# Split Gelu-multiply: the first tile loaded in pieces of 1, 3 and 4 rows instead of 4 and 4, and its first four rows computed in steps of 1 and 3

**Chip, cores, metric.** One core of one Trainium2 chip (trn2). The time is device microseconds of one execution; spans come from the hardware profile of one execution and are 1.8 to 2.4 us shorter than its time.

## The reference

```python
x: (32, 512, 2048) float32
x1, x2 = x[..., :1024], x[..., 1024:]
gelu_x1 = 0.5 * x1 * (1 + erf(x1 / sqrt(2)))
return (gelu_x1 * x2).astype(float32)          # (32, 512, 1024)
```

134.22 MB are read, 67.11 MB written, and there is one Gelu and one multiply for each output element.

## The kernel before

16 tiles; a tile has 128 partitions with 8 rows each, so a load is 8.39 MB (64 KB on each partition) and a store 4.19 MB (32 KB on each partition). There are two buffers for input tiles and two for output tiles. Loads go out on the SyncE queue, stores on the ScalarE queue, except those of the last two tiles, which go out on the SyncE queue.

```python
    xpool = ctx.enter_context(tc.tile_pool(name="xpool", bufs=2))
    opool = ctx.enter_context(tc.tile_pool(name="opool", bufs=2))

    def load(i):
        x_tile = xpool.tile([P, R, dim], x.dtype, name="x_tile")
        for rows in (slice(0, 4), slice(4, 8)) if i == 0 else (slice(0, 8),):
            nc.sync.dma_start(out=x_tile[:, rows, :], in_=x_t[i][:, rows, :])
        return x_tile
    # ... (store() cut)
    ahead = [load(0), load(1)]
    for i in range(n_tiles):
        x_tile = ahead.pop(0)
        o_tile = opool.tile([P, R, half], out.dtype, name="o_tile")
        last = i == n_tiles - 1
        pieces = i == 0 or last
        steps = ((0, 2), (2, 4), (4, 8)) if pieces else ((0, 8),)
        for lo, hi in steps:
            rows = slice(lo, hi)
            # Gelu on ScalarE (kept in program order): o_tile[rows] <- x_tile[rows, :half]
            # multiply on VectorE: o_tile[rows] <- o_tile[rows] * x_tile[rows, half:]
            # ...
            if pieces and hi % 4 == 0:
                store(nc.sync if last else nc.scalar, i, o_tile, slice(hi - 4, hi))
        if not pieces:
            store(nc.sync if i == n_tiles - 2 else nc.scalar, i, o_tile, slice(0, R))
        if i + 2 < n_tiles:
            ahead.append(load(i + 2))
```

## Time and profile before

| | before |
|---|---|
| time, median of 6 runs (lowest to highest) | 471.02 us (470.97 to 471.08) |
| span of the profiled run | 469.2 us |
| bytes moved, mean rate | 201.33 MB, 429 GB/s |
| the two DMA queues, share of 16 engines | 70.4% + 29.1% |
| VectorE / ScalarE busy | 30% / 24% |
| first store issued | 19.28 us |

The fourth and fifth rows are the ones to read together: the transfers fill the span (70.4% + 29.1%), and the engines that compute wait for them. The lines themselves are quoted in the prediction below.

### The profile page before, as it was taken

The numbers are of one execution on the slowest core, as the hardware profiler recorded it, in microseconds if no ns is written. First come the engines' busy times: TensorE is split into PE (matmuls) and PEld (weight loads), VectorE is DVE, ScalarE is ACT, GpSimd is POOL, SyncE is SP. The second block draws the span as 40 slices with busy tenths as digits, with TensorE's granted clock in tenths as the row PEclk, the third lists the DMA queues.
The fourth block names the chain that finished last, engine by engine and source line by source line (L and its number), as shares of the span: only waits on it lengthen the run. The fifth ranks groups of instructions, "written<-read, shape, count | busy, mean of one in ns | idle before, by whom it ended". The sixth has DMA issues, their size and how long they took to land.

```text
span 469.2 us, 182 instructions
## 1 busy us (share of the span) xinstructions
DVE 139.5 (30%) x20; ACT 114.2 (24%) x21; POOL 0.2 (0%) x4
## 2 busy tenths in 40 slices
DVE  0330332407033070330704307042070520605142
ACT  1320505041050410505005050050501405014060
POOL 0000000000000000000000000000000000000000
DMA  8999999999999999999999999999999999999998
GB/s 358 447 447 447 402 400 495 402 402 447 481 413 402 447 402 492 402 422 427 492 402 402 447 481 413 402 447 430 464 402 425 425 492 402 402 447 492 402 402 358
DMA packets 5040, 201.33 MB, mean 429 GB/s; under 512 B 560, under 2 KB 560, under 8 KB 560
## 3 DMA queue, kind: packets, MB, share of 16 engines
q1 hardware_dynamic: 2880, 142.61, 70.4%
q10 hardware_dynamic: 2160, 58.72, 29.1%
HBM read 134.22 MB, written 67.11 MB: 429 GB/s over the span
## 4 chain that ended last, share of the span: by engine, by line
DMA 72%; DVE 14%; ACT 12%; ACTq 0%; SPq 0%; issue 0%
DMA out_dram<-o_tile 62%; DVE o_tile L65 14%; ACT o_tile L61 12%; DMA x_tile<-in_x_dram 10%; ACTq L101 0%; SPq L45 0%
## 5 line engine op out<-in xcount | busy, mean ns | idle before, releaser
L65 DVE TENSOR_TENSOR o_tile<-o_tile,x_tile 128x8192 f32<-128x8192 f32 (+2 forms) x20 | 139.5, 6985 | 321.2 <-ACT o_tile L61 321.2
L61 ACT ACTIVATE o_tile<-x_tile 128x8192 f32<-128x8192 f32 (+2 forms) x20 | 112.9, 5661 | 341.3 <-DMA out_dram<-o_tile 303.6
L61 ACT ACT_TABLE_LOAD x1 | 1.3, 1283 | 0.7 <-PEq L90 0.7
L90 POOL MEMSET const-bfloat16-1.0<- 128x1 bf16 x1 | 0.1, 102 | 0.0
L90 POOL MEMSET const-uint8-127<- 128x1 uint8 x1 | 0.1, 102 | 0.0
L90 POOL MEMSET const-float32-1.0<- 128x1 f32 x1 | 0.1, 99 | 0.0
L90 POOL MEMSET const-float32-0.0<- 128x1 f32 x1 | 0.1, 98 | 0.2 <-issue 0.2
## 6 DMA issues: line engine op xcount, KB each, us to landing
out_dram<-o_tile ACTq DMA_DIRECT2D x13, 4096.0 KB, 42.2
x_tile<-in_x_dram SPq DMA_DIRECT2D x2, 4096.0 KB, 16.7
out_dram<-o_tile ACTq DMA_DIRECT2D x2, 2048.0 KB, 34.4
out_dram<-o_tile SPq DMA_DIRECT2D x1, 4096.0 KB, 22.7
out_dram<-o_tile SPq DMA_DIRECT2D x2, 2048.0 KB, 7.7
x_tile<-in_x_dram SPq DMA_DIRECT2D x15, 42.1
```

Of the source, the lines that this page charges most:

```text
L61: nc.scalar.activation(out=o_tile[:, rows, :], in_=x_tile[:, rows, :half], func=GELU)
L65: nc.vector.tensor_mul(out=o_tile[:, rows, :], in0=o_tile[:, rows, :], in1=x_tile[:, rows, half:],)
L90: nc = _bacc.Bacc("TRN2", target_bir_lowering=False, num_devices=1)
```

## The change

Its intent is to have the first row on the chip earlier, to start computing sooner and so to send the first store sooner. The core of the diff:

```diff
+    FIRST = (0, 1), (1, 4), (4, 8)
...
-        for rows in (slice(0, 4), slice(4, 8)) if i == 0 else (slice(0, 8),):
-            nc.sync.dma_start(out=x_tile[:, rows, :], in_=x_t[i][:, rows, :])
+        for lo, hi in FIRST if i == 0 else ((0, 8),):
+            nc.sync.dma_start(out=x_tile[:, lo:hi, :], in_=x_t[i][:, lo:hi, :])
...
-        steps = ((0, 2), (2, 4), (4, 8)) if pieces else ((0, 8),)
+        if i == 0:
+            steps = FIRST
+        else:
+            steps = ((0, 2), (2, 4), (4, 8)) if last else ((0, 8),)
```

The store of rows 0 to 3 still waits for all four of them.

## The prediction

> **What bounds the kernel now.** I read the page first, its 40 slices and its DMA rows, then the chain that ended last, then the timeline of the first 31 us, where the change acts, then the groups by shape for durations, and last some windows, to see whether the transfers ever pause.
>
> ```profile
> DMA  8999999999999999999999999999999999999998
> GB/s 358 447 447 447 402 400 495 402 402 447 481 413 402 447 402 492 402 422 427 492 402 402 447 481 413 402 447 430 464 402 425 425 492 402 402 447 492 402 402 358
> ...
> q1 hardware_dynamic: 2880, 142.61, 70.4%
> q10 hardware_dynamic: 2160, 58.72, 29.1%
> HBM read 134.22 MB, written 67.11 MB: 429 GB/s over the span
> ```
>
> The DMA engines are at nine tenths or more in 38 of 40 slices, and the two queues together took 70.4 + 29.1 = 99.5% of the 16 engines' span. VectorE (30% on the page) and ScalarE (24%) are mostly idle. So the kernel looks bound by bytes: 201.33 MB.
>
> ```profile
> 1.64 45.41 DMA x_tile<-in_x_dram
> 47.05 0.02 issue
> 47.07 7.04 ACT o_tile L61
> 54.11 0.02 issue
> 54.13 8.70 DVE o_tile L65
> 62.84 0.02 issue
> 62.86 37.73 DMA out_dram<-o_tile
> ```
>
> The chain alternates a transfer, a Gelu, a multiply and a store's landing to the end of the span. It looks like a dependency chain, and one might hope to shorten its first link. But its links of 37 to 45 us are transfers that stand in line behind other transfers: a 4.19 MB store alone would need 9.7 us at 432 GB/s. The steady state has two loads and two stores outstanding, so this chain is the queue's own length, told another way. Whether that is so is decided by whether the DMA ever runs dry, and this is the view that decides it:
>
> ```profile
> 2.00:468.40 466.40, 139.53 (x20) 112.96 (x21) 0.00 (x0) 1.00 1.00 431
> 454.00:466.00 12.00, 5.93 (x2) 2.29 (x1) 0.00 (x0) 1.00 1.01 434
> ```
>
> The columns are stretch, length, busy VectorE, ScalarE and GpSimd, TensorE clock, DMA share, GB/s. The share is 1.00 over all but the first two microseconds and the last one, and it is still 1.01 in the tail, where only stores are left. The trace keeps a record of each packet; following them engine by engine I find no pause longer than 0.06 us on any of the 16 between the first packet, 1.75 us into the span, and the last, which ends at 467.9. So the span is 1.75 us of start, 466.1 us of unbroken transfer, and about 1.3 us after the last packet. The median time of 471.01 us is 1.8 us more than the 469.2 us span.
>
> **The first tile.**
>
> ```profile
> 12.81 3.71 ACT L61 ACTIVATE o_tile<-x_tile 128x2048 f32<-128x2048 f32 x2 [10.80 <-DMA x_tile<-in_x_dram]
> 14.75 4.49 DVE L65 TENSOR_TENSOR o_tile<-o_tile,x_tile 128x2048 f32<-128x2048 f32 x2 [14.75 <-ACT o_tile L61]
> 19.28 0.38 ACTq L49 DMA_DIRECT2D out_dram<-o_tile  x1
> 22.52 3.62 ACT L61 ACTIVATE o_tile<-x_tile 128x4096 f32<-128x4096 f32 x1 [6.00 <-DMA x_tile<-in_x_dram]
> ```
>
> Rows 0 to 3 land at 12.79, and their store is issued at 19.28. Rows 4 to 7 land at 22.50, which is 9.71 us later: 4.19 MB / 9.71 us = 432 GB/s, across a border between two DMAs, so that border cost nothing visible. Until 19.28 the queue is never short of work: the second half of tile 0 and all of tile 1 (8.39 MB, landing at 47.05) wait behind the first piece.
>
> **What the Trainium skill says.** "DMA: Bandwidth & Descriptors", section "Issuing engines are not separate DMA queues", says that DMAs started by any engine run on the same 16 DMA engines and interleave. The trace agrees: the load queue and the store queue add up to 99.5%, so an earlier store takes time from a load. "Perfetto Trace Analysis", section "DMA Optimizations", says that splitting lets work start sooner, and gives as the condition that the DMA engines are generally idle. Here they are not. "ScalarE: Activation LUTs", section "What ACT_TABLE_LOAD costs", gives 186 ns + 0.833 N ns for an activation with immediate scale and bias, 1892 ns at N = 2048; the mean here is 1900. "VectorE: DVE Perf Modes", in its section on the TRN2 errata, gives (N+151)/0.96 ns for an fp32 tensor_tensor, 2291 ns at 2048; the mean here is 2288. Both agree, and I use durations from these rows:
>
> ```profile
> L65 DVE TENSOR_TENSOR o_tile<-o_tile,x_tile 128x2048 f32<-128x2048 f32 x4 | 9.0, 2288 | 30.0 <-ACT o_tile L61 30.0
> L65 DVE TENSOR_TENSOR o_tile<-o_tile,x_tile 128x4096 f32<-128x4096 f32 x2 | 8.9, 4426 | 7.7 <-ACT o_tile L61 7.7
> L61 ACT ACTIVATE o_tile<-x_tile 128x2048 f32<-128x2048 f32 x4 | 7.4, 1900 | 32.8 <-DMA out_dram<-o_tile 22.0 <-DMA x_tile<-in_x_dram 10.8
> L61 ACT ACTIVATE o_tile<-x_tile 128x4096 f32<-128x4096 f32 x2 | 7.2, 3608 | 6.0 <-DMA x_tile<-in_x_dram 6.0
> ```
>
> **The change part by part.** It removes from tile 0 two Gelus and two multiplies of 2048 elements, and adds one of 1024 and one of 3072 on each engine. The lines through the rows above give 192 + 0.834 N ns for the Gelu and 150 + 1.044 N ns for the multiply. So the Gelus become 1.05 and 2.75 us, and the multiplies 1.22 and 3.36 us; the sums, 3.80 and 4.58 us, are those of before (3.80 and 4.58) within rounding, since the instruction count does not change.
>
> Row 0 is a quarter of the first piece: it lands 7.28 us before the four rows did (3.15 MB / 432), at about 5.5 us. Its Gelu and multiply are over by about 7.8 us, 5 us before rows 1 to 3 are there. Those land where the four rows did, at about 12.85. Then Gelu 12.87 to 15.62, multiply 15.64 to 19.00, store issued at about 19.02, against 19.28: **0.26 us earlier**. That small gain is because the multiply of rows 1 to 3 can't start before its whole 3072-element Gelu is through; in the kernel before, the second Gelu ran beside the first multiply. Taking one row out ahead saves 1.05 us of the Gelus after landing and 1.2 us of the multiplies, but loses most of it again by less overlap. The second step of tile 0 waits for its own load at 22.5 and does not move, nor does the third load's issue at about 30.6, which waits for the last multiply of tile 0.
>
> What are 0.26 us worth? While the queue is full, a store that comes sooner only pushes a load's packets back by as much. The total of transfer time is unchanged: **gain on the path 0.0 us**.
>
> Cost: one more load DMA. It brings 128 packets, 8 on each engine, and one small semaphore packet on each. Packets of 16, 32 and 64 KB have medians of 611, 1213 and 2418 ns in the packet records, so doubling the size falls short of doubling the time by about 8 ns: that is the fixed part of a packet. Then 8 and 24 KB take about 310 and 912 ns instead of one of 32 KB at 1213: 9 ns x 8 = 72 ns per engine, plus one semaphore packet of about 9 ns: **+0.08 us**, all of it on the path since no engine pauses. The third issue on the SyncE queue, about 0.4 us, moves tile 1's load from 1.64 to about 2.05; it has 8.39 MB ahead of it, so that is hidden. The sum is 471.01 + 0.08 = 471.1 us.
>
> **Rivals.** (a) *The earlier store carries through to the end*, as the intent and the chain of waits suggest: 471.01 - 0.26 = 470.7 us. For it: the chain starts with the first loads. Against it: DMA share 1.00. (b) *The small first piece breaks the stream*: between the issue at 0.73 us and the landing at 12.79 there are 12.06 us for 9.71 us of bytes, so a start and receipt cost 2.3 us; if a further DMA paid some of it unhidden, 472 to 473 us. Against it: the border between the two pieces now shows no gap, and the second issue is over at about 1.6 us, when the first piece still has some 3 us to run. (c) *A bubble in the tail*: stores get ahead of loads, the last load lands later than 449.05, and the last store (issued at 460.80) finds an empty queue. At 460.80 there were about (467.9 - 460.8) x 432 = 3.07 MB left, of which 2.10 are that last store; the other 0.97 MB are 2.2 us of work, against about 1.0 us from an issue to its first packet (0.73 to 1.75). That leaves 1.2 us of slack; a store that starts 0.26 us earlier can shift the loads by no more than 0.26 us. So no bubble; if there were one, a few tenths at most.
>
> **Range and chances.** All rivals but (b) lie within 0.4 us. The three times of before spread over 0.11 us. I add something for differences between executions: 471.1 us, 470.6 to 471.6. A 2% change is 9.4 us; nothing here is of that size, and the whole time outside unbroken transfer is about 5 us. Same 0.99.
>
> **What would show it.** Right: 5184 packets (4608 of data, 576 small) with 3024 on the load queue, DMA share 1.00 again from 2 us to the end; the first Gelu at about 5.5 us, the 3072-element one at 12.9, first store issued near 19.0; load of tile 1 landing at 47.1 and the last load near 449.1, the span within 0.2 us of 469.2. Wrong: a stretch with a DMA share well under 1 after 2 us, or a span shorter by 0.3 us or more with the first packet no earlier, which would mean that store order does change how much time the same bytes take.

## The result

| | before | after |
|---|---|---|
| median of 6 runs (lowest to highest) | 471.02 us (470.97 to 471.08) | 471.07 us (471.02 to 471.27) |
| span | 469.2 us | 469.1 us |
| DMA packets | 5040 | 5184 |
| first Gelu starts | 12.81 us | 5.64 us |
| first store issued | 19.28 us | 19.10 us |
| tile 1's Gelu starts (its load has landed) | 47.07 us | 47.05 us |

The ratio is 1.0002, with a 95% interval of 0.9989 to 1.0015. A ratio is the mean time of one kernel's fast runs over that of the other's of the same rounds, so it isn't quite the ratio of the medians quoted.

The page of the kernel after, its DMA lines:

```profile
DMA  8999989999999999999999999999999999999998
DMA packets 5184, 201.33 MB, mean 429 GB/s; under 512 B 576, under 2 KB 576, under 8 KB 576
q1 hardware_dynamic: 3024, 142.61, 70.4%
q10 hardware_dynamic: 2160, 58.72, 29.1%
```

The counts 5184, 576 and 3024 are those predicted; the shares of the queues are those of before. The stretches of the prediction, in the kernel after (length, busy VectorE, ScalarE and GpSimd, clock, DMA share, GB/s):

```profile
2.00:468.40 466.40, 139.62 (x20) 113.07 (x21) 0.00 (x0) 1.00 1.00 431
454.00:466.00 12.00, 5.83 (x2) 2.19 (x1) 0.00 (x0) 1.00 1.01 434
```

They are the same in share and rate as before. The timeline of the first tile after (start, length, engine, line, operation; in brackets the idle time before it and what ended it):

```profile
5.64 1.06 ACT L65 ACTIVATE o_tile<-x_tile 128x1024 f32<-128x1024 f32 x1 [3.63 <-DMA x_tile<-in_x_dram]
6.73 1.23 DVE L69 TENSOR_TENSOR o_tile<-o_tile,x_tile 128x1024 f32<-128x1024 f32 x1 [6.73 <-ACT o_tile L65]
12.91 2.76 ACT L65 ACTIVATE o_tile<-x_tile 128x3072 f32<-128x3072 f32 x1 [6.22 <-DMA x_tile<-in_x_dram]
15.71 3.36 DVE L69 TENSOR_TENSOR o_tile<-o_tile,x_tile 128x3072 f32<-128x3072 f32 x1 [7.75 <-ACT o_tile L65]
19.10 0.38 ACTq L50 DMA_DIRECT2D out_dram<-o_tile  x1
22.63 3.62 ACT L65 ACTIVATE o_tile<-x_tile 128x4096 f32<-128x4096 f32 x1 [6.96 <-DMA x_tile<-in_x_dram]
```

The first row is worked on 7.2 us earlier, and of that 0.18 us are left at the store: VectorE stands idle for 7.75 us until the 3072-element Gelu is through. The durations (1.06, 2.76, 1.23, 3.36 us) are those worked out beforehand, within 0.01 us. (The page cited there gives the formula for VectorE for an add; this is a multiply, and its 2288 ns agree with it.)

### The profile page after: what moved, and what is told of

Same layout as the page of the kernel before. It is cut to its first block, busy times and chain, and to the rows that moved or that the text cites. A ratio compares the mean times of both kernels' runs of the same rounds, so it can differ in the third digit from the quotient of the medians.

```text
span 469.1 us, 185 instructions
## 1 busy us (share of the span) xinstructions
DVE 139.6 (30%) x20; ACT 114.3 (24%) x21; POOL 0.2 (0%) x4
## 2 busy tenths in 40 slices
DMA packets 5184, 201.33 MB, mean 429 GB/s; under 512 B 576, under 2 KB 576, under 8 KB 576
## 3 DMA queue, kind: packets, MB, share of 16 engines
q1 hardware_dynamic: 3024, 142.61, 70.4%
## 4 chain that ended last, share of the span: by engine, by line
DMA 72%; DVE 14%; ACT 12%; ACTq 0%; SPq 0%; issue 0%
DMA out_dram<-o_tile 62%; DVE o_tile L69 14%; ACT o_tile L65 12%; DMA x_tile<-in_x_dram 10%; ACTq L105 0%; SPq L46 0%; ACTq L65 0%
## 5 line engine op out<-in xcount | busy, mean ns | idle before, releaser
L69 DVE TENSOR_TENSOR o_tile<-o_tile,x_tile 128x8192 f32<-128x8192 f32 (+4 forms) x20 | 139.6, 6985 | 321.0 <-ACT o_tile L65 321.0
L65 ACT ACTIVATE o_tile<-x_tile 128x8192 f32<-128x8192 f32 (+4 forms) x20 | 113.1, 5662 | 341.1 <-DMA out_dram<-o_tile 303.5
L65 ACT ACT_TABLE_LOAD x1 | 1.3, 1283 | 0.7 <-PEq L94 0.7
```

The source lines that it names most:

```text
L65: nc.scalar.activation(out=o_tile[:, rows, :], in_=x_tile[:, rows, :half], func=GELU)
L69: nc.vector.tensor_mul(out=o_tile[:, rows, :], in0=o_tile[:, rows, :], in1=x_tile[:, rows, half:],)
```

## The experiments

The number had come out, but the prediction's account of it (bytes and packets count, and nothing that happens ahead of a full queue does) could be right for the wrong reason: a gain of the earlier store and a cost of the extra DMA could have cancelled. The first four experiments were made to tell these apart. Their result broke a part of the account, and the other eight follow that up. All 12 kernels gave correct results. By the 2% criterion all are "same" as the kernel before, but for e10 ("unclear"); where I call a kernel slower all the same, the 95% interval of its ratio lies above 1. On this one core the label "slow" of a run goes by its time alone; the clock is 1.0 in all. Runs of one call share a chip and the runs of the kernel before on it; there were 11 of those in each call.

### e1: the change again

No edit. 

> The changed kernel once more, on the chip of the next three. Theory (bytes: the DMA engines never pause, so only bytes and packets count): one more DMA costs 8 x 9 ns of packets and 9 ns of semaphore packet per engine, +0.08 us; time of before + 0.05 to 0.15 us. Rival (two effects that cancel: the store that comes 0.18 us earlier is a gain at the end, and the extra DMA costs about 0.2 us): the same total here, told apart by the next two.

Measured: 471.25 us median, lowest 471.04; but the six runs are 471.05, 471.04, 471.20, 473.27, 471.30 and 473.95. Before: 470.87 to 471.19. The ratio is 1.0020 (1.0001 to 1.0038). Four runs are as expected. Two are 2 to 3 us longer, which neither theory has.

### e2: the loads alone

```diff
 # the change, but
-            steps = FIRST
+            steps = (0, 2), (2, 4), (4, 8)
```

> Loads of tile 0 in 1, 3 and 4 rows, but computed in steps of 2, 2 and 4 as before, so the first store is issued near 19.4 us instead of 19.28 (before) or 19.10 (the change). Bytes: before + 0.08 us, the same as the change. Rival of two cancelling effects: the cost of the DMA without the gain, before + 0.3 us.

Measured: 474.1, 470.9, 483.07, 477.23, 473.88 and 482.82 us; the two near 483 are labelled slow, and the ratio of the other four is 1.0064 (1.0028 to 1.0099). One run is as expected, five are not, and the rival doesn't have 474 to 477 either. The profiled run (474.1 us) is a fast one, and it shows two things. First, the Gelu now waits for two loads, and the load of its function table was placed behind that wait as well: it starts at 12.82 us instead of 0.73, and the first store is issued at 20.58 instead of the 19.4 that I expected. Second, the DMA engines run dry at the end. Stretches of e2 near the end:

```profile
456.00:458.00 2.00, 2.00 (x2) 2.00 (x2) 0.00 (x0) 1.00 0.69 295
458.00:460.00 2.00, 1.66 (x1) 2.00 (x1) 0.00 (x0) 1.00 0.04 16
460.00:462.00 2.00, 1.52 (x1) 0.44 (x1) 0.00 (x0) 1.00 0.95 401
```

and the same stretches of the kernel before:

```profile
456.00:458.00 2.00, 1.68 (x1) 0.29 (x1) 0.00 (x0) 1.00 0.80 344
458.00:460.00 2.00, 2.00 (x1) 0.00 (x0) 0.00 (x0) 1.00 1.03 442
460.00:462.00 2.00, 0.75 (x1) 0.00 (x0) 0.00 (x0) 1.00 0.95 410
```

The share falls to 0.04 while the last multiply is still at work. The chain of waits of e2 says where the delay is from:

```profile
63.12 39.80 DMA out_dram<-o_tile
118.79 42.58 DMA out_dram<-o_tile
177.18 42.82 DMA out_dram<-o_tile
411.83 41.31 DMA out_dram<-o_tile
```

In the kernel before, the same four links start at 62.86, 116.40, 174.47 and 406.81. The starts are when the stores are issued; start and length give the landing. So the store of the first of these links lands 2.3 us late (at 102.92 instead of 100.59), and that of the last 4.1 us late (453.14 instead of 449.05).

The packet records show what set it off. (They don't name the engine; I chained them into 16 engines by letting each packet start where another ends.) In the kernel before, each of the 16 engines takes one 64 KB load packet of tile 1 at about 21.9 us, then the first store packet between 24.37 and 24.79, and from there load and store packets alternate to the end. In e2 14 engines do the same; two take a second 64 KB load packet first, and their first store packet at 27.41 and 27.49. In the end one engine finishes its last 64 KB load packet at 449.16 us, 2.1 us after the last of the other 15 (447.08), and that engine is the only one that never pauses: the 15 others stand still for about 3 us (one of them 1.9) while it catches up and the last rows are computed.

Is the late engine one of the two? The semaphore packets, one of 4 bytes on each engine at the end of each DMA, tell without any chaining. In the kernel before, the 16 engines close the first store together (46.3 to 46.7 us) and the last one of the ScalarE queue too (448.0 to 448.5). In e2, 14 engines close the first store at 46.6 to 47.0 and two at 49.4; and so it goes on through all 15 stores of this queue, up to the last, with 14 at 447.8 to 448.3 and two at 450.6 and 452.8. So the two that missed stay behind to the end. But the lateness of the worse one is not the missed packet alone. The two close tile 3's load ahead of the others (98.9 and 99.0 against 99.8 to 100.2), and only from tile to tile does one of them fall back, until it closes the last load 2.1 us after all others (450.4 against 448.3).

"DMA: Bandwidth & Descriptors", section "Queues, rings and completion order", of the Trainium skill, says that a DMA engine goes round between the queues that it has work for, a packet at a time. The alternation in these records agrees with it, with a difference in what a packet is: the section has typically 9 to 17 descriptors (orders to move one piece of data) in a packet, while here a DMA has 9 records on an engine (8 of data and the semaphore's) and the queues take turns record by record. What that means here is that the moment at which the first store reaches an engine fixes its place in that engine's order. I call that place its slot.

### e3: the steps alone

```diff
 # the change, but
-        for lo, hi in FIRST if i == 0 else ((0, 8),):
+        for lo, hi in ((0, 4), (4, 8)) if i == 0 else ((0, 8),):
```

> Loads of tile 0 in 4 and 4 rows as before, computed in steps of 1, 3 and 4. The Gelus then run 12.8 to 16.6 us and the 3072-element multiply to 20.0, so the first store is issued near 20.0 us, 0.7 us later than before, and no DMA is added. Bytes: before + 0.00 us (within 0.1). Rival (store order carries through to the end): before + 0.7 us.

Measured: 471.05 us median, five runs of 470.94 to 471.08 and one of 473.10. The first store is issued at 20.09, 0.8 us later than before, and the records have it start between 24.46 and 24.97 on all engines: the same slot. The rival's + 0.7 us is not there. In five of six runs 0.8 us of delay ahead of the slot cost nothing; the sixth wasn't profiled.

### e4: the first tile whole

```diff
-    FIRST = (0, 1), (1, 4), (4, 8)
+    FIRST = ((0, 8),)
-        pieces = i == 0 or last
+        pieces = last
```

> Tile 0 loaded, computed and stored whole: one load, one Gelu, one multiply, one store, the first store issued near 38.2 us, 19 us later than before. Bytes: two DMAs, 16 packets per engine and two semaphore packets fewer, so before - 0.16 us, with DMA share 1.00 all the same. Rival (an early first store is worth its time): before + 10 to + 19 us.

Measured: 471.47 us median (471.29 to 471.62), + 0.45 us instead of - 0.16. The timeline of e4:

```profile
22.66 7.03 ACT L65 ACTIVATE o_tile<-x_tile 128x8192 f32<-128x8192 f32 x1 [20.65 <-DMA x_tile<-in_x_dram]
38.44 0.38 ACTq L50 DMA_DIRECT2D out_dram<-o_tile  x1
```

A first store 19.2 us later costs 0.45 us (the interval of the ratio, 0.9996 to 1.0022, includes 1, but no run of e4 is as short as the longest of the kernel before): the strong form of "an early first store is worth its time" is dead. My own figure missed by 0.6 us. The records say where: the packets' own time falls by 0.15 us per engine, as worked out, but the load packets in flight at the first store run longer by 1.0 us per engine, once, against 0.24 us in the kernel before. All engines take the store in the same slot.

### e5: the loads alone, with the table load early

```diff
 # e2, and ahead of the loop a one-element Gelu
+    nc.gpsimd.memset(s_tile[:, 0:1], 0.0)
+    nc.scalar.activation(out=s_tile[:, 1:2], in_=s_tile[:, 0:1], func=GELU)
```

> The loads of the change (1, 3, 4 rows) with the steps of before, as in e2, but a one-element Gelu ahead of everything takes the activation table load to the start (in e2 it came after the loads and put the first store at 20.58 us). First store near 19.4 us. Theory of the slot (what matters is when the first store's packets reach the 16 engines: in e2 14 engines took the first store packet after their first 64 KB load packet, at 24.4 us, and two only one packet later, at 27.4, and those two stayed behind to the end): all 16 take it at 24.4, every run 470.9 to 471.3 us. Rival (the 1, 3, 4 loads themselves cause the slow runs): several of the 6 runs 2 us or more slower, as in e2.

Measured: the table load is at 0.72 us again and the first store at 19.18. The runs are 471.04, 471.19, 471.20, 471.59, 473.03 and 473.87 us. The profiled run (471.59) has all 16 engines in the same slot. So with the store back in its place there are no runs of 477 or 483 in six, as the slot theory has it, but two runs of 473 and more remain, as in e1; the slot theory as I put it ("every run") is not the whole story.

### e6 and e7: the kernel before with a later first store

```diff
 # the kernel before, and ahead of tile 0's first Gelu, into a scratch tile
+            nc.scalar.activation(out=s_tile[:, :, :], in_=x_tile[:, 0:2, :n], func=GELU)
 # e6: n = 725 (1450 elements), e7: n = 1400 (2800 elements)
```

> The kernel before with its loads and steps, only an extra Gelu of 1450 elements into a scratch tile ahead of the first one, so that the first store is issued near 20.6 us, where it was in e2. Slot: some engines miss the slot at 24.4 us; runs of 473 us and more, as in e2. Rival (the 1, 3, 4 loads cause it): every run within 0.3 us of before.

Measured: 471.02 us median; 470.91 to 471.08 and one run of 471.91. First store at 20.62, all engines in the slot at 24.4 to 24.8. This failed for the theory as I had put it: the same store time as in e2 (20.58), and no engine misses. Where exactly the border of the slot lies is therefore different for the two kernels, and I can't say why. Taken together, e5 and e6 say that neither the loads of 1, 3 and 4 rows nor the late store brought a run above 474 us by itself (6 and 5 runs); e2 has both.

> As e6 with 2800 elements: first store near 21.8 us, in the middle of the first 64 KB load packets (21.9 to 24.4). Slot: all 16 engines miss the slot at 24.4 and take the next one near 27 us together; every run within 0.5 us of before. Rival (a later first store costs time in proportion): worse than e6.

Measured: 478.33 us median (477.76 to 478.74), +1.5%, with a first store at 21.75. As expected all 16 engines take the next slot (26.73 to 27.14) together. Against my expectation this costs 7 us, in each of the four runs. The long middle, first the kernel before, then e7:

```profile
47.05:449.05 402.00, 121.69 (x14) 98.41 (x14) 0.00 (x0) 1.00 1.00 432
```

```profile
47.05:449.05 402.00, 121.69 (x14) 98.22 (x14) 0.00 (x0) 1.00 1.00 426
```

The compute is the same and the DMA share is 1.00 in both, yet the rate is 426 GB/s instead of 432. **A DMA share of 1.00 doesn't say that the engines move bytes at their best rate.** The records: between 50 and 440 us the mean 64 KB load packet takes 2472 ns against 2418, because about a fifth of them are stretched, up to 3172 ns in the stretch that I looked at; they come in every tile, about 30 us apart. 53 ns by 108 such packets per engine are 5.8 us; the rest of the 7 us is a pause at the end, as in e2, on some of the engines. In the kernel before, the last packet of a load and the last packet of a store end together on each engine; in e7 the store's last packet, its semaphore's, comes one load packet after that of the load. Why the load packets after it are stretched, no run here shows.

### e8: e2 with a finer last tile

```diff
 # e2, and in the last tile
-            steps = ((0, 2), (2, 4), (4, 8)) if last else ((0, 8),)
+            steps = ((0, 2), (2, 4), (4, 6), (6, 8)) if last else ((0, 8),)
 # with stores of rows 0-3, 4-5 and 6-7
```

> e2 with the last four rows of the last tile computed and stored in two pieces of two rows, so that the last store is half as large and 2.4 us more of other stores stand ahead of it when it is issued. If the loss of e2 is the DMA engines running dry ahead of the last store, each slow run loses up to 2.4 us less: profile without or with a much shorter pause near 458 to 461 us, most runs 471 to 472, the worst (483 in e2) near 480. If the loss lies elsewhere: the same spread as e2.

Measured: 475.9, 479.18 and 480.67 us in the runs labelled fast, and 484.59 to 486.17 in three labelled slow. That is no better than e2. The three fast runs are enough to say that a finer tail doesn't repair e2. The one profile, of a slow run, has six engines, not two, with their first store packet past 27 us; so the number of engines that miss differs between the two profiles, and this run can't tell what the finer tail alone is worth. The idea behind it isn't tested. In that profile the loss isn't at the end anyway: between 47.05 and 449.05 us it moves 421 GB/s (e2: 431, e7: 426, the kernel before: 432), and its mean 64 KB load packet takes 2523 ns. The six engines close the first store 2 us after the other ten (49.2 to 49.5 us against 46.7 to 47.2); by the last one all 16 are spread over 458.2 to 463.0 (448.0 to 448.5 in the kernel before). So in this run, with six engines out of step, those that kept the slot fell behind too.

### e9 and e10: the intent pushed further

```diff
 # e9: the change, but
-            steps = FIRST
+            steps = (0, 1), (1, 2), (2, 4), (4, 8)
 # e10: the change, but
-    FIRST = (0, 1), (1, 4), (4, 8)
+    FIRST = (0, 1), (1, 2), (2, 3), (3, 4), (4, 8)
 # and each piece of tile 0 stored by itself as soon as it is computed
```

> The loads of the change, with the first four rows computed in steps of 1, 1 and 2: first store near 18.1 us, 1.0 us earlier than the change. The intent pushed further. Theory of the phase (in e7 all 16 engines took the first store packet one load packet later, at 26.9 instead of 24.4 us, and from then on the load packets ran about 0.55 us longer in every tile; so it is the store's place in the order of packets, fixed once at the start, that counts, and time saved ahead of the slot counts for nothing): if the packets still start at 24.4, 471.1 us with the change's occasional run of 473; if they start one 32 KB packet earlier, at 21.9, a different order, whose cost I can't tell. Rival (earlier is better): 470 us.

Measured: 472.46 us median (471.85 to 472.54), ratio 1.0028 (1.0016 to 1.0040). The first store is issued at 17.91 us, 1.2 us earlier than in the change, and the kernel is 1.4 us slower than before. 11 of the 16 engines now take the first store packet near 22.6 us, ahead of a 64 KB load packet, and five at 25.2 to 25.4, behind one. The five keep their place as the two of e2 do: they close the first store at 47.6 to 47.9 (the eleven at 44.9 to 45.3) and the last one of the queue at 449.7 to 449.8 (446.2 to 446.5). The last piece of tile 0's load (rows 4 to 7) lands at 23.94 instead of 22.61, and the packets around the first store are stretched by 1.5 us per engine in all (18 to 27 us) against 0.3.

> Each of the first four rows loaded, computed and stored by itself: the first store near 7.8 us, 11 us earlier than the change, at the price of two more loads and three more stores: 40 packets and 5 semaphore packets more per engine at 9 ns, +0.4 us against the change. If only bytes and packets count: 471.5 us. If the order of packets counts: 2 to 10 us more, with load packets longer than 2418 ns in every tile. Rival (earlier is better): 460 us.

Measured: 480.9 us median (480.59 to 481.74), ratio 1.0212 (1.0198 to 1.0225). The first store is issued at 8.02 us, **11 us earlier than in the change, and the kernel is 10 us slower**. The timeline of e10, and two stretches of it:

```profile
92.26 7.03 ACT L65 ACTIVATE o_tile<-x_tile 128x8192 f32<-128x8192 f32 x1 [39.75 <-DMA out_dram<-o_tile]
```

```profile
90.00:100.00 10.00, 0.68 (x1) 7.03 (x1) 0.00 (x0) 1.00 0.98 423
100.00:110.00 10.00, 8.01 (x1) 1.49 (x1) 0.00 (x0) 1.00 0.34 95
```

Tile 2's Gelu starts at 92.26 us (71.62 before), since it has to wait until tile 0's stores have left their buffer, and these take 59 us to land for the last piece and up to 64.6 for a row (28 to 41 in the change). The records show why: a row's store has packets of 4 KB on each engine, and each of them has its turn between two load packets of 32 or 64 KB. So the stores crawl while the loads run ahead, until both input buffers are full, nothing more can be loaded, and the DMA engines stand idle for some 9 us near 100 to 109 us, waiting for a Gelu and a multiply. The rest of the 10 us are the 0.4 us of packets and a stretch of 1.3 us at the restart.

### e11: the change a third time

> The change a third time (12 runs so far: ten between 471.0 and 471.3, two at 473.3 and 474.0; the kernel before: 28 runs, none above 471.32). If the change makes a miss of the slot by single engines more likely, about one run in six is 2 us slower again; if those two were chance of that chip, all six within 0.3 us of before.

Measured: 471.03, 471.04, 471.08, 471.16, 471.17 and 473.22 us, median 471.12; before: 470.87 to 471.21. Of 18 runs of the change (12 on two chips, 6 on one), three are 2 to 3 us long; of the 39 of the kernel before, none (the longest is 471.32). If both had the same rate, the chance that all three fall to the change would be (18 x 17 x 16) / (57 x 56 x 55) = 0.028. That counts in the two runs that had raised the question; e11 alone, made to test it, has one of 6 against none of 11, which says little. So the change probably brings such runs, but in e3 one of six runs did it too, with the loads of before. All three profiled runs of the change were good ones, with all 16 engines in the slot (24.35 to 24.92 us); what the long runs look like inside, I haven't seen. A missed slot on one engine, as in e2, has the right size (one more 64 KB packet is 2.4 us), but that is argued, not shown.

### e12: the first store one packet later still

```diff
 # as e7, with two extra Gelus of 4096 and 1440 elements into rows 4 to 7 of tile 0's output
 # (overwritten by their own Gelu later)
```

> As e7, with the first store at about 24.2 us, one further 64 KB packet later, so that all engines start it near 29.3. If what counts is how many load packets the store trails (none before, one in e7): at least as slow as e7, 478 us or more. If only the trailing by one packet meets the stalls: near 471. If lateness costs in proportion (e7: 7 us for 2.4): 485.

Measured: 472.39 us median (472.33 to 472.73), ratio 1.0031 (1.0019 to 1.0043). The first store is issued at 24.24 and starts between 29.37 and 29.76 on all engines. Later than e7 and 6 us faster (on another chip, where the kernel before takes the same time within 0.05 us): neither lateness nor the number of packets behind orders the times. In the middle e12 runs at the rate of the kernel before:

```profile
47.05:449.05 402.00, 121.69 (x14) 98.01 (x14) 0.00 (x0) 1.00 1.00 432
```

```profile
454.00:466.00 12.00, 8.69 (x3) 5.04 (x2) 0.00 (x0) 1.00 0.87 371
```

```profile
459.08 4.42 DVE L72 TENSOR_TENSOR o_tile<-o_tile,x_tile 128x4096 f32<-128x4096 f32 x1 [0.81 <-ACT o_tile L68]
```

and it loses its 1.3 us at the end, where the share is 0.87: the last multiply starts at 459.08 instead of 456.32, 2.76 us later, and the engines pause for 1.2 to 1.6 us ahead of the last store (one of them 0.8). (The fences are the long middle, the tail, and the last multiply in the timeline.)

No version is faster than the kernel before by more than the noise: the lowest median beside its own kernel before is that of e6 (471.02 against 471.10, ratio 1.0002, 0.9990 to 1.0015), which is the same.

## Why the prediction was right, and where it was not

**The bound, and no gain on the path: right for the change.** The DMA share, the rates and the landing of tile 1 (47.03 against 47.05) and the start of the last tile's Gelu (448.98 against 449.07) are hardly moved. e3 shows it by experiment: a first store 0.8 us later costs nothing while the slot stays the same (five of its six runs).

**The earlier store, 0.26 us: 0.18 us.** The durations were right; the two pieces landed 0.12 and 0.04 us later than I had them (5.62 and 12.89 against 5.5 and 12.85), and the rest are a few hundredths between one instruction and the next.

**The cost, 0.08 us: right in kind, too small to be timed.** The packets of 8 and 24 KB have medians of 309 and 912 ns (estimated 310 and 912), and the sum of all packets at their medians is 465.36 us per engine against 465.29. In the profiled run the stretched packets at the start and at the first store took 0.1 us less than before and hid it. The medians differ by 0.05 us, inside the interval.

**Rival (a), the gain carries through: fell.** e9, which differs from the change in its steps alone, has its first store 1.2 us earlier and is 1.4 us slower than before; e10 has it 11 us earlier than in the change and is 10 us slower than before, but its stores are smaller too.

**Rival (b), the small piece breaks the stream: fell for the profiled runs.** No engine pauses for more than 0.06 us in the profiled runs of e1 and e11; in that of the prediction's own comparison, one pause of 0.36 us on one engine was found, at 2.6 us into the span. The three long runs of the change (473.2 to 474.0 us, where this rival had 472 to 473) left no profile, so for them it isn't excluded.

**Rival (c), a bubble in the tail: the step that failed, though not in the change's profiled runs.** The prediction worked out 1.2 us of slack ahead of the last store, and this held well: in e12 the last store came 2.75 us late and the engines paused for 1.45, so 1.3 us were absorbed; in e2 it came 4.15 us late (the last multiply ends at 464.90 instead of 460.75) and most paused for 3.0 to 3.3, so about 1.0 was absorbed. What failed is the sentence "a store that starts 0.26 us earlier can shift the loads by no more than 0.26 us. So no bubble; if there were one, a few tenths at most". It treats the two queues as one fluid. They are packets in turn: a store that reaches an engine a moment too late waits for a whole 64 KB load packet, 2.4 us, and 16 engines decide this each for itself. When only some of them miss (e2), they stay behind to the end, every landing waits for the slowest, and the bubble is 3 us. When all miss (e7), the order of packets is another one for the whole run, and the transfer itself is slower by 1.4% (426 GB/s against 432). The change stayed in its slot in 15 of 18 runs as far as the times tell, and that is why the number came out. This was partly luck: the prediction had no term for the slot, and could not know that a store 0.18 us earlier stays in it while one 1.4 us earlier (e9) doesn't on 11 engines. The prediction's list of what would make it wrong has the right idea ("store order does change how much time the same bytes take"), but only as a gain.

**What stays open.** What the three long runs of the change look like; why the border of the slot lies elsewhere in e2 and e8 than in e6; why the late engine of e2 falls back from tile to tile; why the packets of e7 are stretched in every tile while those of e12, one packet further behind, are not.

## What to carry to other kernels

When transfers fill the span, expect nothing from working ahead of a full queue; here it bought nothing, and it could cost. The two queues shared the DMA engines packet by packet, so the size of a packet and the moment at which the second queue joined fixed an order that in e2, e7 and e9 lasted to the end. Cutting the first store small gave it the smallest share of the engines just when it should leave quickly (e10). Look at the spread of runs as well as at the median, and compare GB/s between kernels where the DMA share says 1.00.

## What the Trainium skill lacked or had wrong

- "DMA: Bandwidth & Descriptors", section "Queues, rings and completion order", has the turns between queues by packet, which the records here agree with, but not that they give a queue of small packets the smaller share of bytes: in e10 4 KB store packets took turns with 32 and 64 KB load packets, and a store of 0.5 MB needed up to 64.6 us to land. The section also has typically 9 to 17 descriptors in a packet; in these records the queues change over after every record, each of 4 to 64 KB (one partition's piece) or a 4-byte semaphore write, although a DMA has only 9 of them on an engine.
- No page says that the order of the two queues' packets, fixed when the second queue starts, can change the rate of the whole run: 426 GB/s in e7 against 432 in the kernel before and in e12, at a DMA share of 1.00 in all three.
- "Perfetto Trace Analysis", section "DMA Optimizations", says that splitting DMAs may help if the engines are generally idle; it doesn't say that it can cost when they are not, for DMAs above the 2 KB below which the section warns of overhead: +10 us in e10, where the smallest DMA is 0.5 MB.
- "ScalarE: Activation LUTs", section "What ACT_TABLE_LOAD costs", has the 1283 ns that the trace shows, but not that the load is placed behind a wait when its Gelu waits for two loads: 12.82 us in e2 and 12.89 in e8 instead of 0.73, which moved the first store of e2 by 1.3 us.
